# A new model of durations, with a lock for the port pair of VectorE and GpSimd, in the scheduler of an encoder block, and stage priorities chosen with it

## The chip, the cores and the metric

The kernel runs on one core of one Trainium2 chip. The metric is the device time of one launch in microseconds (us). Shorter is better. The engines are TensorE (PE in the rows; its weight loads are PEld), VectorE (DVE), ScalarE (ACT), GpSimd (POOL) and SyncE (SP), whose queue issues all the transfers of this kernel.

## The reference

One layer of a bidirectional encoder on 512 tokens of width 1024, in float32:

```python
x = layer_norm(x, ln_in_g, ln_in_b)
kern = hyena_kernels(feat, t, ...)                 # long-convolution filters from a small network
mixed = parallel_mixer(x, w_in, ...)               # branch A: GLU, depthwise conv 31, LayerNorm, silu, projection
                                                   # branch B: short conv 3, two FFT convolutions with gates, projection
                                                   # y = (g_a * y_a + g_b * y_b) @ w_mix_out
x = layer_norm(DN_ALPHA * x + mixed, ...)
xa = memory_cross_attention(x, mem, wq, wk, wv, wo)   # 4 heads, 256 memory tokens
x = layer_norm(DN_ALPHA * x + xa, ...)
moe = expert_choice_moe(x, w_router, w_gate, w_up, w_down)  # 16 experts, 64 tokens each, width 2048
x = layer_norm(DN_ALPHA * x + moe, ...)
```

The experts' weights are 16 x 3 matrices of 1024 x 2048, 403 MB in all.

## The kernel before

The program is not emitted in the order in which it is written. `body` records every operation (class `Recorder`) with a tag that names its stage; `prepare` gives each an estimated duration (`_cost`) and a critical-path length `bl`; `simulate` is a list scheduler that walks through modelled time and gives each free engine the ready operation of the highest key; `replay` then emits the instructions in that order, each engine in its own queue. As `replay` emits everything from one line, all rows of the profile carry that line (L518 before, L558 after). The names in the rows are buffers: `v` a virtual tile, `h` a piece of a host unit, `ident`, `ones`, `iota` constants.

The key of an operation is

```python
o.key = -o.i if o.late else 1e6 + o.bl - 1e-4 * o.i + prio.get(o.tag, 0)
```

so the table `PRIO` shifts whole stages, and the late part, the experts, runs in the order of the code. Some operations have alternatives (`alts`). `vg` lets an elementwise operation on two SBUF tiles go to VectorE or GpSimd, and `cp` lets a copy go to ScalarE or VectorE; `elsewhere` decides whether the engine at hand should leave the operation to the other. `split` makes the two halves of a number for three-product matmuls: a copy (`cp`) into the high half, then a subtraction (on VectorE if the source is PSUM, else by `vg`).

The stages that matter here, by their tags:

- memory keys `mt`, `mk0` to `mk7`; input LayerNorm `l0` to `l3`; filter network `fn`; filters `k00` to `k11`; DFT matrices `kd`, `df`.
- hyena inputs `c8.*`, `c0.*`; forward transforms and products in the frequency domain `f00` to `f11`, inverses `i00` to `i11`; the short convolution of the second gate `x0` to `x3`.
- GLU `g0` to `g3`; depthwise convolution `d0` to `d3`: per channel tile 24 SCALAR_TENSOR_TENSOR of about 500 columns on VectorE (`SIDE` = 3 taps on either side go to ScalarE, whose results GpSimd adds, five additions per tile); its LayerNorm `cl`.
- sixteen sigmoid gates `t0` to `t15`, each a product with a 1024 x 128 piece of `w_in`, whose weights are split first and whose result is stored to DRAM.
- projections of the two branches `b8` to `b15` (hyena) and `b0` to `b7` (conformer), eight products of 12 matmuls each; mixing `mx0`, `mx1`; LayerNorm `lm*`; values `mu`, `mv0`, `mv1`; attention `q*`, `s*`, `p*`, `o*`; output projection `wo0`, `wo1`; router `r00` to `r31`; top-k and what follows `tk`.

Every piece of weights that goes through `weight` is loaded by SP, split into a ring of four units, and used by TensorE. The expert stage streams 384 loads of 1 MB through the units of SBUF that are free; an expert needs 24. The first of these loads are issued before the front part is over, as units come free, and the rest as TensorE gives units back.

Of the kernel before, what the change touches and what calls it, by code (L numbers as in the profile page):

```python
# [31 lines left out]
PRIO = {"": 32, "b0": -50, "b1": -429, "b10": 94, "b11": -35, "b12": 27, "b13": -31, "b14": 62, "b2": -500, "b3":  # L32
# [60 lines left out]
class Op:  # L93
    __slots__ = ("i", "alts", "rd", "wr", "preds", "succ", "bl", "key", "tiles", "late", "tag", "claims")
# [78 lines left out]
def _free(ap):  # L173
    n = 1
    for st, c in list(ap.ap)[1:]:
        n *= c
    return n


def _cost(alt, psum):  # L180
    eng, meth, args, kw = alt
# [3 lines left out]
    if eng == "SP":  # L185
        b = 4 * int(np.prod([c for _, c in o.ap]))
        return b / 360e3
    if meth == "matmul":
        n = _free(o)
        r32 = x.dtype == F32R  # L190
        c = n / 2400 if r32 else max(4 * n, 512) / 2400
        k, m = x.shape[0], _free(x)
        return c / 2 if not r32 and (k == 64 or m == 64) else c
# [12 lines left out]
    return 0.068 + n * 1.0417e-3 + 0.06 * ptr  # L206

# [53 lines left out]
def prepare(rec):  # L261
# [32 lines left out]
    for op in ops:  # L294
        psum = any(v.cls in "BP" for v, _ in op.rd + op.wr)
        op.alts = [(a[0], _cost(a, psum), a) for a in op.alts]
    for op in reversed(ops):
        e = op.alts[0][0]
        tail = max([s.bl + min(_lat(e, f[0]) for f in s.alts) for s in op.succ.values()] or [0.0])
        op.bl = min(c for _, c, _ in op.alts) + tail + (2.0 if e == "SP" else 0.0)  # L300
# [4 lines left out]
def simulate(rec, prio, n=None):  # L305
# [32 lines left out]
    table, dma = [0], [0.0]  # L338
# [30 lines left out]
    def elsewhere(o, a, t):  # L369
        mine = t + o.alts[a][1]  # L370
        for b, (f, c, _) in enumerate(o.alts):
            if b != a:
                w = max(free[f], t, rtime[o.i][b]) + c
# [9 lines left out]
    def start(o, a, t):  # L383
# [11 lines left out]
        else:  # L395
# [5 lines left out]
            if e == "PE":  # L401
# [4 lines left out]
                c = c + 0.003 if clock[1] else 2 * c  # L406
                w, x = clock[0], t
                while x < t + c:
                    y = min(t + c, (w + 1) * WINDOW)
                    busy[w] = busy.get(w, 0.0) + y - x  # L410
                    w, x = w + 1, y
            fin = t + c
# [1195 lines left out]
```

## Time and profile before

| what | value |
| --- | --- |
| time before, median of 3 runs | 1681.75 us (1680.91 to 1682.41) |
| time of the profiled execution | 1678.9 us |
| its span, first to last instruction | 1677.1 us |
| busy TensorE / VectorE / ScalarE / GpSimd | 1481.5 / 739.6 / 278.0 / 273.7 us |
| granted TensorE clock, mean | 0.953 |
| bytes moved by transfers | 474.41 MB |

A row of the profile gives the busy time of a group of instructions, the mean of one, and the idle time of its engine just before them with what ended it. Outside the span lie 1.8 us of the profiled execution.

### The profile page before, as it was taken

What the parts mean: (1) busy time and instruction counts of PE and PEld (TensorE: products, weight loads), DVE (VectorE), ACT (ScalarE), POOL (GpSimd) and SP (SyncE); (2) the same over time, 40 slices, a digit from 0 to 9 for tenths busy, and PEclk for the clock granted to TensorE, in tenths of its full rate; (3) what the DMA queues carried; (4) which work ended last, traced back from release to release, by engine and by line L of the source; (5) the groups of instructions that cost most, each with busy time, mean ns of one, the idle gap of its engine ahead of it and who ended that gap; (6) DMA issues with size and microseconds to landing.
All of it is one profiled execution on the core that took longest, in us unless ns stands there. A gap on an engine that the chain in (4) does not pass through costs nothing.

```text
span 1677.1 us, 17272 instructions
## 1 busy us (share of the span) xinstructions
PE 1481.5 (88%) x6998; PEld 806.1 (48%) x6998; DVE 739.6 (44%) x1018; ACT 278.0 (17%) x465; POOL 273.7 (16%) x161
## 2 busy tenths in 40 slices
PE   7789886687899998699999999999989989988885
PEld 5678674466777887543443434324224224222222
DVE  7998999879767654603111111101101111110115
ACT  3323252123113232111100100001001001000001
POOL 3662467745101000002000000000000000000002
PEclk9889998788999998899999999999999999999997
DMA  8312221223623335579999999999999999999993
GB/s 293 130 50 90 99 64 53 67 76 107 200 89 125 114 134 209 222 301 421 415 415 419 417 415 417 418 415 416 419 415 415 420 416 414 419 417 415 418 409 149
DMA packets 99319, 474.41 MB, mean 283 GB/s; under 512 B 8449, under 2 KB 8961, under 8 KB 66344
## 3 DMA queue, kind: packets, MB, share of 16 engines
q1 hardware_dynamic: 99240, 473.31, 71.6%
q8 instruction: 55, 0.90, 0.2%
q14 instruction: 24, 0.20, 0.0%
HBM read 463.84 MB, written 9.44 MB: 282 GB/s over the span
## 4 chain that ended last, share of the span: by engine, by line
PE 52%; DMA 23%; DVE 18%; issue 3%; POOL 2%; ACT 1%; SPq 0%; DVEq 0%; ACTq 0%; POOLq 0%
PE v L518 52%; DVE v L518 14%; DMA v<-in_moe_w_down_dram 10%; DMA v<-in_moe_w_gate_dram 6%; DMA v<-in_moe_w_up_dram 6%; DVE h L518 4%; POOL v L518 2%; ACT v L518 1%; ACT h L518 0%; POOL h L518 0%; DMA h<-in_mem_dram 0%; DMA h<-in_conf_out_dram 0%; DMA h<-in_w_in_dram 0%; SPq L518 0%; DVEq L1604 0%
## 5 line engine op out<-in xcount | busy, mean ns | idle before, releaser
L518 PE MATMUL v<-v,v 128*64 128x512 f32 (+5 forms) x6370 | 1395.7, 487 | 117.5 <-DMA v<-in_moe_w_down_dram 30.4
L518 PEld LDWEIGHTS v<-v,v 128*128 128x128 f32 (+2 forms) x6370 | 729.7, 168 | 750.6 <-issue 440.2
L518 DVE TENSOR_TENSOR v<-v,v 128x512 f32<-128x512 f32 (+3 forms) x263 | 213.4, 841 | 695.0 <-PE v L518 629.3
L518 ACT ACTIVATE v<-v 128x512 fp32r<-128x512 f32 (+6 forms) x168 | 99.8, 598 | 925.3 <-PE v L518 889.0
L518 POOL TENSOR_TENSOR v<-v,mhalf 128x1 f32<-128x1 f32 (+2 forms) x21 | 15.6, 771 | 1101.3 <-DVE v L518 1101.3
L518 POOL TENSOR_TENSOR v<-h,v 128x1024 fp32r<-128x1024 f32 (+1 forms) x35 | 104.7, 2997 | 43.4 <-ACT v L518 39.3
L518 DVE SCALAR_TENSOR_TENSOR v<-v,v,v 128x499 f32<-128x499 f32 (+14 forms) x116 | 109.2, 1003 | 1.9 <-ACT v L518 1.8
L518 DVE TENSOR_TENSOR v<-h,v 128x1024 fp32r<-128x1024 f32 (+2 forms) x81 | 94.0, 1172 | 23.5 <-ACT v L518 20.9
L518 ACT ACTIVATE v<-h 128x1024 fp32r<-128x1024 f32 (+2 forms) x78 | 73.9, 961 | 131.9 <-PE v L518 89.9
L518 POOL TENSOR_TENSOR v<-v,v 128x512 f32<-128x512 f32 (+3 forms) x19 | 44.8, 2365 | 144.7 <-ACT v L518 89.9
L518 ACT ACTIVATE v<-v,v 128x128 f32<-128x128 f32 (+1 forms) x72 | 30.5, 494 | 149.2 <-PE v L518 125.8
L518 ACT ACTIVATE h<-v,v 128x512 f32<-128x512 f32 (+4 forms) x68 | 42.5, 660 | 68.7 <-PE v L518 61.3
L518 PE MATMUL v<-ident,v 128*128 128x128 f32 (+1 forms) x292 | 44.4, 287 | 9.7 <-DVE v L518 9.5
L518 DVE TENSOR_TENSOR v<-v 128x512 f32<-128x512 f32 (+4 forms) x50 | 50.6, 1056 | 1.2 <-POOL v L518 1.1
L518 PEld LDWEIGHTS v<-ident,v 128*128 128x128 f32 (+1 forms) x292 | 33.2, 145 | 36.5 <-issue 27.2
L518 PE MATMUL v<-ident,h 128*128 128x128 f32 (+1 forms) x116 | 19.4, 320 | 32.6 <-DVE h L518 20.2
L518 POOL TENSOR_TENSOR h<-h 128x256 f32<-128x256 f32 (+4 forms) x29 | 43.5, 1507 | 25.3 <-ACT h L518 17.2
L518 DVE TENSOR_SCALAR v<-iota,v,v 128x128 f32<-128x128 f32 x64 | 18.4, 343 | 63.9 <-PE v L518 63.9
L518 DVE CAST v<-h 128x1024 fp32r<-128x1024 f32 (+1 forms) x36 | 25.9, 725 | 25.1 <-PE v L518 14.9
L518 DVE COPY v<-v 128x256 f32<-128x256 f32 (+1 forms) x33 | 14.3, 433 | 47.2 <-ACT v L518 43.8
L518 PEld LDWEIGHTS v<-ident,h 128*128 128x128 f32 (+1 forms) x116 | 17.0, 184 | 35.2 <-issue 18.7
L518 DVE SCALAR_TENSOR_TENSOR v<-v,v 128x512 f32<-128x512 f32 (+1 forms) x28 | 16.9, 620 | 34.9 <-PE v L518 34.8
(67 smaller groups left out, 403.3 us busy)
## 6 DMA issues: line engine op xcount, KB each, us to landing
v<-in_moe_w_gate_dram SPq DMA_DIRECT2D x128, 1024.0 KB, 19.9
v<-in_moe_w_up_dram SPq DMA_DIRECT2D x128, 1024.0 KB, 20.0
v<-in_moe_w_down_dram SPq DMA_DIRECT2D x128, 1024.0 KB, 20.2
h<-in_w_in_dram SPq DMA_DIRECT2D x36, 512.0 KB, 3.6
v<-h SPq DMA_DIRECT2D x20, 256.0 KB, 2.1
h<-in_wk_dram SPq DMA_DIRECT2D x8, 512.0 KB
v<-v SPq DMA_DIRECT2D x8, 512.0 KB
v<-v SPq DMA_DIRECT2D x4, 1024.0 KB, 6.6
```

The source lines that it names most:

```text
L518: getattr(engs[e], meth)(*[fix(x) for x in args], **{k: fix(x) for k, x in kw.items()})
```

## The change

Four things change in the planner; `body`, `replay` and the work itself stay.

1. `_cost`: a transfer is priced at 418 instead of 360 bytes per ns, a float32r matmul 13 ns longer, a float32 one 6 ns longer (and 3 ns less in `simulate`).
2. A lock. `_shares` tells which alternatives use the port pair that VectorE and GpSimd have in common: on GpSimd every operation with two wide operands or more, on VectorE those with two inputs outside PSUM and copies and TENSOR_SCALARs between SBUF tiles. `simulate` keeps the time at which the lock is free, and an operation that shares it starts its work then.
3. `elsewhere` adds the wait for the lock to the cost of the engine at hand, and a penalty `GPEN` per tag to the GpSimd alternative; 1000 keeps a stage off GpSimd.
4. `PRIO` has new values (two lines of some thirty are shown).

```diff
-PRIO = {"": 32, "b0": -50, "b1": -429, "b10": 94, "b11": -35, "b12": 27, "b13": -31, "b14": 62, "b2": -500, "b3":
+PRIO = {"": 5334.6553, "b0": -4277.89, "b1": -5870.442, "b10": 1996.3081, "b11": 2057.3843, "b12": -8116.7025,
...
+GPEN = {"b0": 1000, "b10": -1.2595, "b13": 2.5939, "b14": 1000, "b2": 1000, "b4": 1000, "b5": 1000, "b6": 2.4193,
...
-        return b / 360e3
+        return b / 418e3
...
-        c = n / 2400 if r32 else max(4 * n, 512) / 2400
+        c = n / 2400 + 0.013 if r32 else max(4 * n, 512) / 2400 + 0.006
...
+def _shares(alt):
+
+    eng, meth, args, kw = alt
+    wide = [y for y in args if isinstance(y, bass.AP) and _free(y) > 2]
+    if eng == "G":
+        return len(wide) > 1
+    if eng != "V" or len(wide) < 2:
+        return False
+    src = [y for y in wide[1:] if y.tensor.name not in _BANKS]
+    if meth in ("tensor_tensor", "scalar_tensor_tensor", "match_replace"):
+        return len(src) > 1
+    return meth.startswith(("tensor_scalar", "tensor_copy")) and len(src) == 1 and wide[0].tensor.name not in _BANKS
...
     def elsewhere(o, a, t):
-        mine = t + o.alts[a][1]
+        pen = GPEN.get(o.tag, 0.0)
+        mine = t + o.alts[a][1] + (max(0.0, port[0] - t) if o.port[a] else 0.0)
+        mine += pen if o.alts[a][0] == "G" else 0.0
         for b, (f, c, _) in enumerate(o.alts):
             if b != a:
-                w = max(free[f], t, rtime[o.i][b]) + c
+                w = max(free[f], t, rtime[o.i][b]) + c + (pen if f == "G" else 0.0)
...
-                c = c + 0.003 if clock[1] else 2 * c
+                c = c if clock[1] else 2 * c
...
+            if o.port[a]:
+                c += max(0.0, port[0] - t)
+                port[0] = t + c
```

What this does to the program, counted over its operations. Call first part all stages up to the end of `cl` and `i11` (everything that precedes the projections of the branches). In it 76 elementwise operations move from GpSimd to VectorE (28 of 1024 columns into float32r, 28 of 512 float32, 12 of 256, 4 of 512 into float32r, 4 of 1024 float32), and 14 move from VectorE to GpSimd (3 of 1024, 5 of 512 float32, 2 of 512 into float32r, 4 of 256). Copies: 19 move from VectorE to ScalarE (8 of 1024, 10 of 512, 1 of 256), 9 the other way (6 of 1024, 3 of 512). GpSimd's tile operations there go from 113 to 51: 7 of 1024, 20 of the depthwise convolution, 12 of 512, 12 of 256. In the part from the projections to the router GpSimd has 4 before and 4 after. In the late part 9 operations of 512 go from GpSimd to VectorE, four of them in the last LayerNorm.

GpSimd's queue in the depthwise convolution, before. The 128x511 to 128x509 rows are its additions; the 128x1024 rows are the subtractions of `split` for weights of `t` and `x` stages, in the ring buffers `v401`, `v321`, `v409`, `v324`, `v373`:

```order
L518 TENSOR_TENSOR h20_80<-h20_80,h21_85 128x510
L518 TENSOR_TENSOR v401_1767<-h24_82,v401_1767 128x1024
L518 TENSOR_TENSOR h20_80<-h20_80 128x509
L518 TENSOR_TENSOR v321_1795<-h23_78,v321_1795 128x1024
L518 TENSOR_TENSOR h20_80<-h20_80 128x509
L518 MEMSET h22_87 128x1
L518 TENSOR_TENSOR h22_87<-h22_87,h21_85 128x511
L518 TENSOR_TENSOR v409_1843<-h24_82,v409_1843 128x1024
L518 TENSOR_TENSOR h22_87<-h22_87,h21_85 128x510
L518 TENSOR_TENSOR h22_87<-h22_87,h20_80 128x510
L518 TENSOR_TENSOR v324_1883<-h23_78,v324_1883 128x1024
```

The same queue after, at the end of that stage:

```order
L558 TENSOR_TENSOR h21_122<-h21_122,h22_132 128x509 x2
L558 MEMSET h21_122 128x1
L558 TENSOR_TENSOR h21_122<-h21_122,h20_80 128x511
L558 TENSOR_TENSOR h21_122<-h21_122 128x510
L558 TENSOR_TENSOR h21_122<-h21_122,h22_132 128x510
L558 TENSOR_TENSOR v330_2048<-h23_78,v330_2048 128x1024
L558 TENSOR_TENSOR h21_122<-h21_122,h22_132 128x509
L558 TENSOR_TENSOR h21_122<-h21_122,h20_80 128x509
L558 TENSOR_TENSOR v397_2140<-h23_78,v397_2140 128x1024
```

Of the weight splits in this stage two are left on GpSimd, `v330` (stage `x3`) and `v397` (stage `t1`). The others stand on VectorE, between the SCALAR_TENSOR_TENSORs of the convolution (`v266` is its result; `v413`, `v417` are ring buffers of `t` stages):

```order
L558 SCALAR_TENSOR_TENSOR v266_1858<-v265_1651,v0_111,v266_1858 128x503
L558 TENSOR_TENSOR v413_2231<-h23_78,v413_2231 128x1024
L558 SCALAR_TENSOR_TENSOR v266_1858<-v265_1651,v0_111,v266_1858 128x503
L558 SCALAR_TENSOR_TENSOR v266_1858<-v265_1651,v0_111,v266_1858 128x506
L558 SCALAR_TENSOR_TENSOR v266_1858<-v265_1651,v0_111,v266_1858 128x502
L558 SCALAR_TENSOR_TENSOR v266_1858<-v265_1651,v0_111,v266_1858 128x505
L558 SCALAR_TENSOR_TENSOR v266_1858<-v265_1651,v0_111,v266_1858 128x502
L558 SCALAR_TENSOR_TENSOR v266_1858<-v265_1651,v0_111,v266_1858 128x505
L558 SCALAR_TENSOR_TENSOR v266_1858<-v265_1651,v0_111,v266_1858 128x501
L558 TENSOR_TENSOR v417_2270<-h23_78,v417_2270 128x1024
```

TensorE's queue at the projections, before. Products with `v348` and `v355` are the hyena branch's (`b8` to `b15`), those with `v444` and `v445` the conformer's (`b0` to `b7`):

```order
L518 MATMUL v429_2772<-v355_2722,v428_2764 128x512
L518 MATMUL v486_2811<-v444_2683,v483_2782 128x512
L518 MATMUL v486_2811<-v445_2693,v483_2782 128x512
L518 MATMUL v486_2811<-v444_2683,v483_2782 128x512 x2
L518 MATMUL v486_2811<-v445_2693,v483_2782 128x512
L518 MATMUL v486_2811<-v444_2683,v483_2782 128x512 x2
L518 MATMUL v486_2811<-v445_2693,v483_2782 128x512
L518 MATMUL v486_2811<-v444_2683,v483_2782 128x512 x2
L518 MATMUL v433_2827<-v348_2567,v432_2820 128x512 x2
```

After, all hyena products stand ahead of the conformer's, and the matmuls of `cl` (with `ones`) among them:

```order
L558 MATMUL v433_2750<-v355_2703,v432_2724 128x512
L558 MATMUL v455_2777<-ones_70,h20_80 128x1 x4
L558 MATMUL v433_2750<-v355_2703,v432_2724 128x512 x5
L558 MATMUL v430_2726<-v355_2703,v428_2719 128x512 x2
L558 MATMUL v459_2796<-h20_80,ones_70 128x128 x4
L558 MATMUL v430_2726<-v355_2703,v428_2719 128x512 x2
L558 MATMUL v429_2806<-v348_2643,v428_2719 128x512 x6
L558 MATMUL v429_2806<-v355_2703,v428_2719 128x512 x6
L558 MATMUL v442_2826<-v348_2643,v441_2753 128x512 x6
```

In the late part SP issues its 392 transfers in the same order as before, and TensorE's products follow the order of the code more closely (gathers of later experts no longer stand inside the products of an earlier one).

## Rows read from the trace of the kernel before

**Rows 1.** The page: span, busy time of three engines with their share and count, and transfers in 40 equal slices of 41.9 us.

```profile
span 1677.1 us, 17272 instructions
...
PE 1481.5 (88%) x6998; PEld 806.1 (48%) x6998; DVE 739.6 (44%) x1018; ACT 278.0 (17%) x465; POOL 273.7 (16%) x161
...
GB/s 293 130 50 90 99 64 53 67 76 107 200 89 125 114 134 209 222 301 421 415 415 419 417 415 417 418 415 416 419 415 415 420 416 414 419 417 415 418 409 149
```

**Rows 2.** Busy time of each engine in five stretches: the first part, the projections, mixing to top-k, experts, the end. Columns: stretch, its length, busy us of PE, PEld, DVE, ACT, POOL with counts, granted TensorE clock, DMA share, GB/s.

```profile
0.00:432.00 432.00, 341.68 (x1662) 279.81 (x1662) 389.86 (x441) 136.08 (x189) 241.89 (x136) 0.89 0.32 105
432.00:484.00 52.00, 46.14 (x196) 36.41 (x197) 39.14 (x53) 7.59 (x9) 3.52 (x2) 1.00 0.45 148
484.00:715.60 231.60, 206.69 (x1013) 170.22 (x1013) 142.14 (x236) 53.16 (x110) 10.74 (x10) 0.93 0.43 155
715.60:1640.00 924.40, 870.27 (x3996) 310.13 (x3998) 145.84 (x250) 77.36 (x152) 8.42 (x5) 0.99 1.01 412
1640.00:1677.10 37.10, 16.70 (x134) 9.56 (x130) 22.57 (x40) 3.80 (x6) 9.13 (x8) 0.79 0.31 118
```

**Rows 3.** The chain that ended last, at the projections and before top-k. Columns: start us, length us, what.

```profile
432.30 3.66 DMA h<-in_conf_out_dram
...
436.82 42.52 PE v L518 x183
...
481.27 1.30 DVE v L518 x2
...
482.60 1.23 DVE v L518
...
483.88 5.29 PE v L518 x15
```

```profile
695.78 1.86 DVE v L518 x10
```

**Rows 4.** Instructions in order of time around the start of the expert stage: TensorE's first gather product, and SP's issues (start us, time until the last of the group was issued).

```profile
715.64 1.65 PE L518 MATMUL v<-v,v 128*128 128x128 f32 x6 [1.04 <-DVE v L518]
```

```profile
693.85 36.76 SPq L518 DMA_DIRECT2D v<-in_moe_w_gate_dram  x8
732.00 14.10 SPq L518 DMA_DIRECT2D v<-in_moe_w_down_dram  x8
```

**Rows 5.** VectorE's instructions by shape in 0 to 432 us. Columns: names, shapes, count, busy us, mean ns of one, idle time before them.

```profile
L518 DVE TENSOR_TENSOR v<-v 128x512 f32<-128x512 f32 x32 | 36.2, 1176 | 1.2 <-POOL v L518 1.1
...
L518 DVE TENSOR_TENSOR v<-v,v 128x1024 f32<-128x1024 f32 x12 | 27.6, 2350 | 0.1
L518 DVE SCALAR_TENSOR_TENSOR v<-v,v,v 128x507 f32<-128x507 f32 x8 | 14.9, 1865 | 0.0
...
L518 DVE TENSOR_TENSOR v<-h,v 128x512 fp32r<-128x512 f32 x15 | 14.7, 1002 | 2.4 <-PE v L518 1.5 <-ACT v L518 0.7
...
L518 DVE SCALAR_TENSOR_TENSOR v<-v,v,v 128x508 f32<-128x508 f32 x8 | 11.7, 1464 | 1.0 <-ACT v L518 1.0
...
L518 DVE SCALAR_TENSOR_TENSOR v<-v,v,v 128x504 f32<-128x504 f32 x8 | 11.1, 1398 | 0.0
L518 DVE TENSOR_TENSOR h<-v,h 128x512 f32<-128x512 f32 x16 | 10.6, 680 | 0.7 <-PE v L518 0.7
L518 DVE TENSOR_TENSOR h<-h,h 128x512 f32<-128x512 f32 x8 | 10.5, 1315 | 0.7 <-ACT h L518 0.7
...
L518 DVE TENSOR_TENSOR v<-v 128x1024 f32<-128x1024 f32 x8 | 9.7, 1213 | 0.0
...
L518 DVE SCALAR_TENSOR_TENSOR v<-v,v,v 128x500 f32<-128x500 f32 x8 | 5.8, 730 | 0.0
```

**Rows 6.** GpSimd's instructions in 0 to 432 us by operands: min/median/max ns of one, first and last start, shapes; and one group by shape (as in rows 5).

```profile
L518 POOL TENSOR_TENSOR v<-h,v x33: 1287/2700/17238, 20.9 to 423.6; 128x1024 fp32r<-128x1024 f32 x28, 128x512 fp32r<-128x512 f32 x5
...
L518 POOL TENSOR_TENSOR h<-h,h x16: 1277/1596/2142, 61.5 to 396.1; 128x510 f32<-128x510 f32 x7, 128x512 f32<-128x512 f32 x4, 128x511 f32<-128x511 f32 x3, 128x509 f32<-128x509 f32 x2
L518 POOL TENSOR_TENSOR v<-v x14: 1182/1298/1779, 162.1 to 398.5; 128x512 f32<-128x512 f32 x12, 128x256 f32<-128x256 f32 x2
```

```profile
L518 POOL TENSOR_TENSOR h<-h 128x256 f32<-128x256 f32 x18 | 18.3, 1030 | 7.9 <-DVE h L518 7.3 <-POOL h L518 0.2
```

**Rows 7.** Instructions in order of time in the depthwise convolution, and the first two waits of VectorE. Columns: start us, length us, instruction, count, in brackets the idle time before it and what ended it.

```profile
305.38 23.95 DVE L518 SCALAR_TENSOR_TENSOR v<-v,v,v 128x511 f32<-128x511 f32 x33 [0.54 <-ACT v L518]
...
314.29 19.57 POOL L518 TENSOR_TENSOR v<-h,v 128x1024 fp32r<-128x1024 f32 x2 [4.38 <-ACT v L518]
...
331.58 16.67 PE L518 MATMUL v<-v,v 128*128 128x512 f32 x60 [14.25 <-POOL v L518]
...
345.38 1.23 DVE L518 TENSOR_TENSOR v<-h,v 128x1024 fp32r<-128x1024 f32 x1 [16.05 <-ACT v L518]
```

```profile
4.48 0.69 DVE L518 CAST v<-h 128x1024 fp32r<-128x1024 f32 x1 [4.48 <-DMA h<-in_wk_dram]
...
10.02 0.69 DVE L518 TENSOR_TENSOR v<-v,v 128x512 fp32r<-128x512 f32 x1 [3.59 <-ACT v L518]
```

**Rows 8.** Instructions in order of time in the last LayerNorm.

```profile
1662.51 6.49 POOL L518 TENSOR_TENSOR v<-v,v 128x512 f32<-128x512 f32 x4
...
1662.96 1.58 DVE L518 TENSOR_TENSOR v<-v,v 128x512 f32<-128x512 f32 x1
...
1666.13 3.41 DVE L518 TENSOR_TENSOR v<-v,v 128x512 f32<-128x512 f32 x2
```

More of the change, by code (lines that the diff above doesn't have):

```diff
@@ L93 @@
 class Op:
-    __slots__ = ("i", "alts", "rd", "wr", "preds", "succ", "bl", "key", "tiles", "late", "tag", "claims")
+    __slots__ = ("i", "alts", "rd", "wr", "preds", "succ", "bl", "key", "tiles", "late", "tag", "claims", "port")
 class Engine:
@@ L206, in _cost @@
     return 0.068 + n * 1.0417e-3 + 0.06 * ptr
+def _shares(alt):
[9 more added lines that the diff above has]
+    return meth.startswith(("tensor_scalar", "tensor_copy")) and len(src) == 1 and wide[0].tensor.name not in _BANKS
+_BANKS = set()
 def _lat(a, b):
@@ L295, in prepare @@
         psum = any(v.cls in "BP" for v, _ in op.rd + op.wr)
+        _BANKS.update(v.name for v, _ in op.rd + op.wr if v.cls in "BP")
         op.alts = [(a[0], _cost(a, psum), a) for a in op.alts]
+        op.port = [_shares(a) for _, _, a in op.alts]
     for op in reversed(ops):
@@ L337, in simulate @@
     clock, busy = [0, False], {}
-    table, dma = [0], [0.0]
+    table, dma, port = [0], [0.0], [0.0]
     order, ev, rel = [], [0.0], []
```

39 rows, old and new, of tables (GPEN, PRIO) are left out of this document.

## The prediction

> **What bounds the kernel now.** Read the transfers in slices first [rows 1]: from slice 18 to the end they move 409 to 421 GB/s, a flat line, and before it half of that at most but for the first slice and the last two. The table of stretches [rows 2] says the same: 1.01 of the transfer engines in 715.6 to 1640 us, 0.32 to 0.45 before. So the kernel has a part bound by the experts' weights (924 us, 412 GB/s) and a front part of 716 us that isn't bound by transfers. Is the front hidden behind the stream? No: SP spends 36.76 us on the eight gate loads of the second expert, and the next load goes out at 732.0 [rows 4], since those units come free only when TensorE works on the first expert, after its first gather product at 715.64 [rows 4]. Whatever the front part loses or gains before 715.64 moves the end by as much.
>
> The front part has two halves. To 432 us VectorE is busy 389.9 us of 432 and TensorE 341.7 at a granted clock of 0.89 [rows 2]. From 484 to 715.6 TensorE is busy 206.7 of 231.6 [rows 2] and the last 16 us of it are top-k on VectorE. Between them stand the projections: the chain runs on TensorE from 436.82 for 42.5 us and, after a short turn over VectorE, reaches the first mixing product at 483.88 [rows 3]. So the change can act in one place above all, VectorE's first 432 us.
>
> **What VectorE's 389.9 us consist of.** Shapes whose operands leave GpSimd little to collide with have steady prices: 0.68 us for 512 columns, 1.21 for 1024, 0.73 for a step of the depthwise convolution [rows 5]. The same shapes cost more elsewhere: 32 of 512 columns 1.18, 12 of 1024 columns 2.35, convolution steps 1.87, 1.46, 1.40 [rows 5]. What exceeds the steady price is 16 us in the 32, 13.7 in the 12, 9.1, 5.9 and 5.3 in those three groups of convolution steps, 5.1 and 4.9 in two groups of TENSOR_TENSORs [rows 5]; the same subtraction over all groups of that view gives 106 us. VectorE's own work is then 390 - 106 = 284 us. GpSimd was busy 242 us meanwhile [rows 2], 232 of them in 113 tile operations, so a microsecond of GpSimd costs VectorE 106/232 = 0.46. GpSimd pays too: its 1024-column subtraction takes 17.2 us at worst against a median of 2.7 [rows 6]. That one did harm: while VectorE ran 33 convolution steps in a row, GpSimd's split waited, TensorE stood 14.25 us for it, and VectorE then 16.05 us for a copy of weights behind that [rows 7].
>
> **The change, part by part.**
>
> *Work moved onto VectorE.* 32 operations of 1024 columns at 1.21, 32 of 512 at 0.68 and 12 of 256 at 0.4 (estimate: just over half of the 512 price) come, 65 us; 3, 7 and 4 of them go, 10 us; the copies exchanged with ScalarE take off about 6 (19 go, 9 come, 0.4 to 1.2 each). That is +49 us; 52 more instructions in the queue, and neighbours overlap by some 0.06 us (32 x 1.176 is 37.6, busy 36.2 [rows 5]), so +46. Nine operations of later stages stand ahead of the last of `cl`: +7. Own work 284 + 46 + 7 = 337 us. All of this is on the path, as VectorE is what bounds this half.
>
> *Collisions, taken away and left.* GpSimd keeps 51 tile operations there: 7 of 1024 at 2.70, 20 additions at 1.60, 12 of 512 at 1.30, 12 of 256 at 1.03 [rows 6], 81 us. At 0.46 that costs VectorE 37 us; by the count, 106 x 51/113, it is 48. I take 40, near the first, as the price per microsecond is the better measure. The bounds are 0 (all of it where VectorE works from PSUM or waits) and 81 (each microsecond costs one). The Trainium skill, SBUF — State Buffer, Who interferes with whom, calls the shared port pair an exclusive lock for the whole instruction, where the second to issue waits until the first is done; by that alone each side waits for one instruction of the other at most. The 17.2 us under 33 steps [rows 6, 7] say that here GpSimd lost the pair many times in a row. By the page's rule the term has the upper bound of 81, and the sum below would come out at 487 instead of 446.
>
> *Idle time of VectorE.* It was 432 - 389.9 = 42.1 us: 8.1 at the start, for the first weights and the first copy [rows 7], 16.05 behind the starved split [rows 7], 18 in small waits. After: 8 and 18 stay, the 16 go, as the splits of that stage stand on VectorE but for two. New is about 16: the gates `t` now come before the second transforms, so TensorE has nothing to fill in during `f10` to `cl`, and its granted clock, 0.89 on average in this half [rows 2], can fall to its lower level of 1.2 GHz. I put 7 us on that (some 14 us of products of `f1*` and `i1*` that VectorE waits for, half as long again), and 9 us on the turns of `cl` over TensorE and ScalarE (two reductions, one broadcast, one sigmoid, some 2 us each), which other work covered before; both are estimates. 34 us in all beside the start; bounds 18 and 45.
>
> *The projections.* They took 484 - 432 = 52 us after VectorE had finished the first half, as all 192 products came behind it. After, the hyena branch's 96 stand ahead, among the matmuls of `cl`, and 96 remain: 96 x 42.5/183 = 22 us, with 2.6 of VectorE behind them [rows 3] and 2 for the clock, 27. Their weights' splits and products on VectorE are about as long (25 us) and lie beside.
>
> Sum for the first mixing product: before 8 + 34 + 390 + 52 = 484; after 8 + 337 + 40 + 34 + 27 = 446. **38 us earlier.**
>
> *Mixing to top-k*: the same 1,000 matmuls, four GpSimd operations before and after. At the end two more router chains stand behind the last output projection, 1.9 us each on VectorE [rows 3], but TensorE gets there earlier by the products that it leaves for later: 0, within 3 either way.
>
> *Expert stage*: SP's order is unchanged and the stream ran at its flat rate with both kinds of order on TensorE, for the first two experts stood in the new kind already: 0. In the last LayerNorm four operations on GpSimd, 6.49 us, go to VectorE at 0.68 and no longer stretch its own of 1.58 and 3.41 [rows 8]: 0. The prices of transfers and matmuls act through the order alone.
>
> So the span goes from 1677.1 to 1639, the profiled execution from 1678.9 to 1641. The median of the runs shown stands 2.85 us above that execution; 1681.75 - 38 = 1644.
>
> **Rivals.**
>
> *The split starves again.* Two splits are left on GpSimd in the convolution, `x3` and `t1`, under the same steps on VectorE. For it: the planner's lock hands over after each operation, the trace shows 33 in a row [rows 7]. Against it: VectorE's queue there is now mixed with subtractions that wait for ScalarE's copies and let GpSimd in. Price: about 15 us each (17.2 less the undisturbed 2.4, TensorE's wait of 14.25 [rows 7]): 1659 with one, 1674 with both.
>
> *Collisions nearly vanish.* The early GpSimd work falls where VectorE reads PSUM, at 10 to 15 us for the term instead of 40, and the new idle time stays away: some 40 us more, 1604 to 1612.
>
> *VectorE is only loaded more (slower).* GpSimd's work left lies in the convolution and the filters, where VectorE's steps read SBUF twice, and each microsecond costs more than one, as a VectorE instruction that loses also delays what ScalarE and TensorE wait for. The sum turns at a term of 78 us; at the 106 of before it gives 512 for the first mixing product, 28 late: 1710, and at 95, 1699. A page speaks for it in part: the Trainium skill, Perfetto Trace Analysis, Optimizing Scalar/DVE Operations, says that where VectorE is saturated offloading to other engines may make sense, and adds that between these two it may not help. VectorE at 390 of 432 us is that case, and the change goes the other way; the 106 us say that offloading didn't pay here.
>
> *No change.* The front is shorter, but the expert stream starts no earlier, because units come free late. [Rows 4] speak against it: the loads wait for the first products alone.
>
> **Chances.** The forecast, 25 to 55 us faster: 0.47. Starvation again, 4 to 25 faster: 0.21. More than 55: 0.14. No change: 0.06. Slower: 0.12. A measurement tells 0.2% (3.4 us) from no change: faster 0.82, same 0.06, slower 0.12. The range of 1612 to 1680 leaves out about 0.19: the slower case and half of the upper one. The likeliest one's own range is 1627 to 1657.
>
> **What would show it.** VectorE's busy time to the end of `cl` near 370 us; its 512- and 1024-column groups near 0.68 and 1.21; GpSimd near 80 us there, no weight split of 10 us or more; the first mixing product at 446, the first gather near 678; the stream flat from there on, 961 us to the end. Wrong would be: convolution steps above 1.2 us on average, VectorE idle over 60 us before the projections, or a dip below 409 GB/s in the expert stage.

## The result, and the profile after

The changed kernel takes 1621.88 us (median; 1619.88 to 1624.72) against 1681.33 (1680.32 to 1682.41) for the kernel before on the same chip: a ratio of 0.9648, 95% interval 0.9631 to 0.9664. That is 59.5 us less where 38 were forecast: the sign and the range held, the size didn't. Ratios in this text are against executions of the kernel before in the same session, whose medians lie between 1679.1 and 1681.3 us; in two sessions 5 of 24 of these executions took only 1669 to 1674 us, as 3 of 10 of "old, `mv0` late" below took 1668 to 1669, and since none of them was profiled the reason is open. The page of the kernel after:

```profile
span 1620.4 us, 17237 instructions
...
PE 1459.3 (90%) x6998; PEld 792.9 (49%) x6998; DVE 699.4 (43%) x1076; ACT 288.2 (18%) x478; POOL 112.7 (7%) x90
...
GB/s 306 120 64 93 103 104 136 104 69 158 78 91 169 26 337 207 229 418 414 418 418 415 418 418 415 418 418 416 417 418 415 417 419 415 418 419 415 417 408 153
```

GpSimd's 273.7 us have become 112.7, and VectorE's busy time fell by 40 us although it has 58 instructions more [rows 1]. The flat part of the transfers is as before, 414 to 419 GB/s but for the last two slices (408 in the last but one, 409 before). Next the kernel after in the five stretches of [rows 2], with the same columns (stretch, length, busy us of PE, PEld, DVE, ACT, POOL with counts, clock, DMA share, GB/s); the borders are now the end of `cl`, the first mixing product, the first gather, and 37 us from the end:

```profile
0.00:407.80 407.80, 345.44 (x1741) 288.10 (x1742) 367.15 (x502) 149.45 (x204) 96.72 (x75) 0.90 0.38 125
407.80:437.46 29.66, 26.36 (x114) 21.02 (x113) 27.30 (x43) 4.45 (x5) 0.00 (x0) 0.99 0.21 71
437.46:659.70 222.24, 204.39 (x1016) 169.49 (x1017) 141.32 (x235) 53.24 (x111) 13.33 (x11) 0.95 0.45 161
659.70:1583.40 923.70, 864.33 (x3978) 303.37 (x3980) 142.77 (x255) 77.24 (x152) 0.00 (x0) 0.99 1.01 412
1583.40:1620.40 37.00, 18.82 (x154) 10.95 (x150) 20.85 (x44) 3.81 (x6) 2.67 (x4) 0.82 0.34 131
```

Against [rows 2, 3]: the first mixing product comes at 437.46 instead of 483.88 (46.4 us earlier), the stretch from there to the first gather takes 222.2 instead of 231.8 (9.5 less), and from the first gather to the end it is 960.7 against 961.5. Together 56.7 us of span (the profiled execution of before is 2.4 us under its median, hence less than 59.5). The first two terms are nearly the whole effect, 55.9 us.

The chain that ended last around the projections (start, length, what), to be held against [rows 3]:

```profile
396.41 37.77 PE v L558 x166
...
434.20 0.70 DVE h L558
...
436.11 1.31 DVE v L558 x2
...
437.46 12.77 PE v L558 x41
```

TensorE is now on the chain from before the end of `cl`: its 166 products to 434.2 hold the last projections of both branches, in place of 183 products that began some 5 us after VectorE was through.

VectorE's instructions by shape up to 407.8 us (columns as in [rows 5]):

```profile
L558 DVE TENSOR_TENSOR v<-h,v 128x1024 fp32r<-128x1024 f32 x48 | 63.1, 1314 | 3.5 <-PE v L558 2.7 <-ACT v L558 0.5
L558 DVE TENSOR_TENSOR v<-v 128x512 f32<-128x512 f32 x44 | 33.5, 814 | 0.0
L558 DVE TENSOR_TENSOR v<-v,v 128x1024 f32<-128x1024 f32 x16 | 18.7, 1219 | 0.0
...
L558 DVE SCALAR_TENSOR_TENSOR v<-v,v,v 128x501 f32<-128x501 f32 x8 | 8.0, 999 | 0.0
...
L558 DVE SCALAR_TENSOR_TENSOR v<-v,v,v 128x508 f32<-128x508 f32 x8 | 7.3, 914 | 0.0
...
L558 DVE SCALAR_TENSOR_TENSOR v<-v,v,v 128x502 f32<-128x502 f32 x8 | 6.7, 835 | 0.0
...
L558 DVE SCALAR_TENSOR_TENSOR v<-v,v,v 128x507 f32<-128x507 f32 x8 | 5.9, 735 | 0.0
```

In [rows 5] the 512-column group cost 1176 ns each, the 1024-column one 2350, the 507-column step 1865. Now 44 of the first take less than 32 did, the second is at its steady 1.2 us, and only three groups of convolution steps are still well above 0.73 us (999, 914 and 835 ns). The splits of weights that came over (`v<-h,v`, 48 in all) cost 1.31 each.

GpSimd's splits over the same time (count, min/median/max ns, first and last start, shapes), against the 33 with a worst case of 17238 in [rows 6]:

```profile
L558 POOL TENSOR_TENSOR v<-h,v x12: 1286/2398/4935, 28.8 to 386.5; 128x1024 fp32r<-128x1024 f32 x8, 128x512 fp32r<-128x512 f32 x4
```

### The profile page after: what moved, and what is told of

It is laid out like the page before. It is cut to its first block, busy times and chain, and to the rows that moved or that the text cites. A ratio compares the mean times of both kernels' runs of the same rounds, so it can differ in the third digit from the quotient of the medians.

```text
span 1620.4 us, 17237 instructions
## 1 busy us (share of the span) xinstructions
PE 1459.3 (90%) x6998; PEld 792.9 (49%) x6998; DVE 699.4 (43%) x1076; ACT 288.2 (18%) x478; POOL 112.7 (7%) x90
## 4 chain that ended last, share of the span: by engine, by line
PE 61%; DMA 26%; DVE 7%; ACT 1%; POOL 1%; issue 0%; DVEq 0%; SPq 0%; ACTq 0%
PE v L558 61%; DMA v<-in_moe_w_up_dram 10%; DMA v<-in_moe_w_down_dram 8%; DMA v<-in_moe_w_gate_dram 6%; DVE v L558 6%; DVE h L558 1%; POOL v L558 1%; ACT v L558 1%; DMA h<-in_w_mix_dram 0%; DMA h<-in_w_in_dram 0%; ACT h L558 0%; POOL h L558 0%; DVEq L1644 0%; SPq L558 0%; ACTq L558 0%
## 5 line engine op out<-in xcount | busy, mean ns | idle before, releaser
L558 PE MATMUL v<-v,v 128*64 128x512 f32 (+5 forms) x6370 | 1376.9, 486 | 103.8 <-DMA v<-in_moe_w_down_dram 33.3
L558 PEld LDWEIGHTS v<-v,v 128*64 128x64 f32 (+2 forms) x6370 | 719.2, 167 | 728.5 <-issue 416.3
L558 ACT ACTIVATE v<-v 128x512 fp32r<-128x512 f32 (+5 forms) x175 | 104.5, 606 | 882.1 <-PE v L558 846.6
L558 DVE TENSOR_TENSOR v<-h,v 128x1024 fp32r<-128x1024 f32 (+1 forms) x101 | 119.6, 1190 | 10.4 <-PE v L558 5.0
L558 DVE SCALAR_TENSOR_TENSOR v<-v,v,v 128x498 f32<-128x498 f32 (+14 forms) x116 | 82.5, 758 | 5.4 <-ACT v L558 5.2
L558 POOL TENSOR_TENSOR v<-h,v 128x1024 fp32r<-128x1024 f32 (+1 forms) x15 | 38.8, 2586 | 146.4 <-ACT v L558 146.3
L558 PEld LDWEIGHTS v<-ident,v 128*128 128x128 f32 x292 | 32.8, 143 | 31.1 <-issue 17.8
L558 PE MATMUL v<-ident,v 128*128 128x128 f32 x292 | 43.7, 285 | 2.9 <-DVE v L558 2.9
L558 ACT ACTIVATE h<-v 128x512 f32<-128x512 f32 (+3 forms) x35 | 17.8, 514 | 102.9 <-PE v L558 102.6
L558 POOL TENSOR_TENSOR h<-h,h 128x509 f32<-128x509 f32 (+3 forms) x18 | 27.6, 1535 | 79.0 <-ACT h L558 77.5
```

Of the source, the lines that this page charges most:

```text
L558: getattr(engs[e], meth)(*[fix(x) for x in args], **{k: fix(x) for k, x in kw.items()})
```

## Experiments

Four terms recur. T is the end of `cl` or `i11`, whichever is later. VectorE's *excess* up to T is what its instructions took over their steady price (0.68 us for 512 columns, 1.21 for 1024, 0.73 for a convolution step, and so on), summed over the instructions matched one by one with the plan; that gives 110 us before, where the prediction's sum over groups gave 106. *Own* is busy time less excess, *idle* is T less busy. The last projection ends with its last operation outside TensorE, and the last column goes to the first step of top-k on VectorE. The table has all the runs; the sections after it say what each was for.

| kernel | time, us | T | own | excess | idle | GpSimd busy to T | T to last projection | from there to top-k |
| --- | --- | --- | --- | --- | --- | --- | --- | --- |
| before | 1681.3 | 431 | 279 | 110 | 42 | 242 | 51 | 218 |
| after | 1621.9 | 408 | 333 | 34 | 41 | 97 | 29 | 207 |
| old order, new engines | 1646.8 | 396 | 329 | 38 | 30 | 89 | 53 | 220 |
| new order, old engines | 1658.9 | 443 | 286 | 95 | 62 | 218 | 30 | 208 |
| 16 splits to VectorE | 1655.5 | 406 | 297 | 85 | 25 | 179 | 52 | 218 |
| 2 splits to VectorE | 1682.3 | 433 | 282 | 107 | 45 | 236 | 51 | 218 |
| GpSimd least | 1652.2 | 433 | 360 | 19 | 54 | 43 | 33 | 210 |
| no lock in the plan | 1666.8 | 426 | 337 | 47 | 42 | 99 | 53 | 210 |
| no penalties | 1695.2 | 485 | 294 | 97 | 94 | 218 | 28 | 208 |
| old priorities | 1691.8 | 444 | 311 | 59 | 74 | 160 | 54 | 218 |
| old, `mv0` late | 1676.7 | 430 | 280 | 108 | 42 | 242 | 52 | 215 |
| new, `mv0` early | 1632.2 | 407 | 334 | 34 | 40 | 96 | 29 | 219 |

### Engines alone, order alone

The kernel before with its order, but each of the 107 operations that stand on another of VectorE and GpSimd in the kernel after put there (`SWAP` maps an operation's number to its alternative); and the reverse, the kernel after with these operations put back. The copies that the change exchanges between VectorE and ScalarE (19 and 9 in the first part) are not among the 107: they go with the order in both runs.

```diff
+SWAP = {43: 0, 71: 0, 100: 1, 128: 0, 157: 0, 242: 0, 369: 0, 372: 0, 382: 1, 385: 1, 388: 0, 390: 1, 399: 1,
...
-    return sorted(order)
+    return [(t, i, SWAP.get(i, a)) for t, i, a in sorted(order)]
```

> The order of the kernel before, unchanged on every queue, with each of the 107 operations that the change moves between VectorE and GpSimd on the engine that it has after. Theory A (fewer collisions between VectorE and GpSimd are the gain): VectorE's own work rises by some 46 us to 333, collisions fall from 106 to 35, the 16 us behind the starved split go, so the first part ends 30 to 40 us earlier than 432, the projections (52 us) and the mixing part stay: 1642 to 1652 us. Theory B (the new order is the gain): no gain, 1677 to 1727, as VectorE has more of its own work.

Measured: 1646.79 us, ratio 0.9809 [0.9794, 0.9824], 32 us less. The row to the end of `i11` (columns as in [rows 2]):

```profile
0.00:395.80 395.80, 332.43 (x1646) 271.42 (x1647) 366.33 (x503) 136.55 (x188) 88.92 (x74) 0.92 0.34 113
```

The engines alone bring VectorE to the same 366 us of busy time as after (367), and it is through at 396, 12 us before the kernel after. What this kernel lacks comes later: 53 us of projections instead of 29, and 220 us to top-k instead of 207.

> The order of the kernel after with the 107 operations on the engines that they had before. Theory A: collisions return to about 106 us and own work falls by 46, so the first part ends 25 to 40 us later than 408: 1647 to 1662 us. Theory B: 1617 to 1627, as after.

Measured: 1658.93 us, 0.9886 [0.9871, 0.9901], 19 us less by the ratio (20 by the medians). VectorE is later (443 against 431) with 62 us idle, but the projections and the part behind them are as short as after. So the two halves of the change act in two places: the engines on VectorE up to T, the order (with the copies) on what lies behind T, and the order costs 12 us at T with either assignment (396 to 408, 431 to 443).

### Which work to take off GpSimd

The kernel before with only the 16 splits of 1024 columns of the `t` and `x` stages moved to VectorE, by the same code; and with only two of them, one in `x3` and one in `t6`, which I took for the pair behind which TensorE had stood 14.25 us [rows 7]. They are not that pair, as the time lines below show.

```diff
+SWAP = {1616: 0, 1646: 0, 1676: 0, 1706: 0, 1920: 0, 1949: 0, 1978: 0, 2007: 0, 2065: 0, 2094: 0, 2123: 0,
+        2181: 0, 2210: 0, 2268: 0, 2326: 0, 2355: 0}
```

> The kernel before, with only the 16 subtractions of 1024 columns in the weight splits of the t and x stages moved from GpSimd to VectorE. Theory A: 16 x 1.15 = 18 us more of own work, about 59 us of GpSimd less at 0.46 = 27 us fewer collisions, no stall of 16 us behind a starved split: 25 us faster, 1656. Theory B: 1681 to 1699. If the starved split alone matters: near 1680, since 16 won and 18 spent.

Measured: 1655.53 us, 0.986 [0.9845, 0.9874], 24 us less: these 16 operations give three quarters of what the engines alone give (14 of them are among the 76 that the change moves; the other two, in `x3` and `t1`, it leaves on GpSimd). Excess falls by 25, own work grows by 18, and idle time falls by 17: the 16 us behind the starved pair are gone.

```diff
+SWAP = {1706: 0, 2326: 0}
```

> The kernel before, its order kept; of the whole change only two subtractions of 1024 columns (one each in x3 and t6, the pair behind which TensorE stood 14.25 us and VectorE then 16.05 us) move from GpSimd to VectorE. Theory (the starved pair costs that idle time by itself): VectorE's idle time before the projections falls from 42 to 26 to 30 us, its own work grows by 2.4, and the time falls by 11 to 16 us, to 1665 to 1670. Rival (the next split left on GpSimd starves in its place, so only the move of all sixteen helps): idle time stays at 38 to 44 us and the time at 1678 to 1684.

Measured: 1682.3 us, 1.0019 [1.0002, 1.0037], within 0.2% of the kernel before. The kernel before has four weight splits in a row on GpSimd at this place. By the plan the first two are those of `t6` and `x3`, which took 5.74 us together (start, length, instruction, count, idle time before it):

```profile
304.18 5.74 POOL L518 TENSOR_TENSOR v<-h,v 128x1024 fp32r<-128x1024 f32 x2 [1.85 <-ACT v L518]
```

The starved pair behind them, at 314.29 [rows 7], is that of `t14` and `t13`. In this run `t6` and `x3` stand on VectorE and the starved pair is still on GpSimd. The time line of VectorE, then of GpSimd:

```profile
305.81 1.22 DVE L520 TENSOR_TENSOR v<-h,v 128x1024 fp32r<-128x1024 f32 x1 [0.88 <-ACT v L520]
...
308.92 1.21 DVE L520 TENSOR_TENSOR v<-h,v 128x1024 fp32r<-128x1024 f32 x1
310.06 20.91 DVE L520 SCALAR_TENSOR_TENSOR v<-v,v,v 128x504 f32<-128x504 f32 x32
347.35 1.23 DVE L520 TENSOR_TENSOR v<-h,v 128x1024 fp32r<-128x1024 f32 x1 [16.38 <-ACT v L520]
```

```profile
315.67 19.84 POOL L520 TENSOR_TENSOR v<-h,v 128x1024 fp32r<-128x1024 f32 x2 [11.93 <-ACT v L520]
```

So the time came out as the rival said, but the run tests neither the theory nor the rival. It is the same pair as before that starves: 17.50 us for its first split, 19.84 for both, and VectorE idles 16.38 us. Whether moving this pair alone would have saved the 11 to 16 us stays open. The nearest to a test is the run with 16 splits, which moves it along with 14 others: idle time fell by 17 us. What the two splits do show is that splits that don't starve are worth nothing on either engine (3 us more of own work, 3 us less excess). The first split of the pair ends 2.2 us after the last of the 32 steps: it is done when the run is over.

### As little as possible on GpSimd

The kernel after, where the plan pays 1000 us for any alternative on GpSimd.

```diff
-        pen = GPEN.get(o.tag, 0.0)
+        pen = 1000.0
```

> The kernel after with the penalty of 1000 for every stage: GpSimd keeps only the 20 additions of the depthwise convolution. 31 operations more on VectorE are 21 us of its own work; some 65 us of GpSimd less at 0.35 to 0.45 are 23 to 29 us fewer collisions: 1612 to 1625, near after. If GpSimd's remaining work was hidden (its collisions where VectorE waits anyway): 1635 to 1645.

Measured: 1652.21 us, 0.9846 [0.9813, 0.988], 30 us slower than after. Excess falls to 19 us, but own work grows to 360 and idle time to 54. Own work and excess together are 379 against 367: the last 54 us of GpSimd cost 15 us of excess and save 27 us of work. The plan also has another order here, with 13 us more of idle time and 7 us more behind T; what in it costs them was not taken apart.

### The plan's rules, one at a time

The kernel after without the lock in the plan; without the penalties; and with the old table of priorities. Each lets the planner make a new order and a new assignment.

```diff
-        op.port = [_shares(a) for _, _, a in op.alts]
+        op.port = [False for _ in op.alts]
```

> The kernel after with the lock taken out of the planner (no operation shares the pair) and the penalties and priorities kept; GpSimd gets 57 tile operations in the front instead of 55. If the price per microsecond of GpSimd (0.35 to 0.47) is what counts: 1620 to 1630, as the engines are nearly those of after. If the lock's place in the plan counts for itself, as it tells the planner when a slot is free: 1635 to 1650.

Measured: 1666.84 us, 0.9927 [0.9902, 0.9952]. GpSimd has hardly more to do than after (99 us), since the penalties keep work off it; excess is 47, idle time 42. Of the 45 us lost against after, 24 are in the projections: `i11` ends after `cl` in this order, and 53 us follow T. Another 19 are lost up to T.

```diff
-GPEN = {"b0": 1000, "b10": -1.2595, "b13": 2.5939, "b14": 1000, "b2": 1000, "b4": 1000, "b5": 1000, "b6": 2.4193,
...
+GPEN = {}
```

> The kernel after with the penalties on GpSimd taken out and the lock and priorities kept; GpSimd gets 117 tile operations again. If its amount of work is what counts: 62 operations more, some 120 us, cost 50 us of collisions and spare VectorE 46 us, and the starved or late splits come on top: 1640 to 1660. If the lock in the plan is enough: 1620 to 1630.

Measured: 1695.17 us, 1.0097 [1.0059, 1.0135]: slower than the kernel before. With the lock in the plan, but no penalty, GpSimd gets 218 us of work again. In order of time:

```profile
327.14 21.81 DVE L551 SCALAR_TENSOR_TENSOR v<-v,v,v 128x511 f32<-128x511 f32 x30 [5.10 <-ACT v L551]
...
329.81 2.94 POOL L551 TENSOR_TENSOR v<-h,v 128x1024 fp32r<-128x1024 f32 x1 [4.59 <-ACT v L551]
...
338.56 14.91 POOL L551 TENSOR_TENSOR v<-h,v 128x1024 fp32r<-128x1024 f32 x2 [5.81 <-ACT v L551]
...
351.20 13.65 PE L551 MATMUL v<-v,v 128*128 128x512 f32 x46 [11.93 <-POOL v L551]
...
371.55 2.99 DVE L551 TENSOR_TENSOR v<-v 128x512 f32<-128x512 f32 x3 [22.60 <-PE v L551]
```

Thirty steps in a row, a starved pair of splits, TensorE 11.93 us late, VectorE 22.60. A split that came early in the same run got in at once, for 2.94 us, and cost VectorE one step of 2.86 instead of 0.73; the next one lost until the run was over. What decides between the two, these records don't show. The plan's lock has each side wait for one operation of the other, as in the first case. So it doesn't see what starvation costs. That the penalties are what keeps the splits away from it in the kernel after is likely by this run, though the order differs too.

```diff
-PRIO = {"": 5334.6553, "b0": -4277.89, "b1": -5870.442, "b10": 1996.3081, "b11": 2057.3843, "b12": -8116.7025,
...
+PRIO = {"": 32, "b0": -50, "b1": -429, "b10": 94, "b11": -35, "b12": 27, "b13": -31, "b14": 62, "b2": -500, "b3":
...
```

> The kernel after with the table of priorities of before; lock, penalties and prices new. GpSimd gets 73 tile operations. From the run with old order and new engines (32 us faster) and 22 operations more on GpSimd: 1640 to 1655, with the wait of TensorE for the last head's softmax still there. If lock and prices find as good an order by themselves: 1620 to 1635.

Measured: 1691.75 us, 1.0083 [1.0051, 1.0116], slower than before too: idle time 74. GpSimd's longest splits (time line):

```profile
332.51 18.20 POOL L550 TENSOR_TENSOR v<-h,v 128x1024 fp32r<-128x1024 f32 x2 [11.48 <-ACT v L550]
...
368.27 12.23 POOL L550 TENSOR_TENSOR v<-h,v 128x1024 fp32r<-128x1024 f32 x1 [16.32 <-ACT v L550]
```

### The 9.5 us between mixing and top-k

TensorE's time line in the kernel before, at the softmax of the last head:

```profile
632.60 2.02 PE L518 MATMUL v<-ident,h 128*128 128x128 f32 x8 [4.24 <-DVE h L518]
635.31 0.79 PE L518 MATMUL v<-v,v 128*128 128x512 f32 x1 [0.69 <-ACT v L518]
636.64 8.71 PE L518 MATMUL v<-v,v 128*128 128x512 f32 x28 [0.53 <-DVE v L518]
```

It waits 5.5 us in three places, and 28 matmuls then take 8.71 us. The 20 us around it (columns as in [rows 2]), and behind it the 20 us at the same stage after:

```profile
623.88:643.88 20.00, 13.99 (x59) 10.78 (x58) 8.58 (x15) 5.27 (x13) 0.00 (x0) 0.74 0.73 288
```

```profile
577.46:597.46 20.00, 20.00 (x93) 16.34 (x92) 11.66 (x21) 4.77 (x10) 0.00 (x0) 1.00 1.02 408
```

A granted clock of 0.74 over 20 us is half clock, 1.2 GHz, for 10.2 of them (the records have it from 630.9 to 641.1). After, TensorE has products of `o0` and `o1` left, since the value product `mv0` on which they wait has a very low priority; it doesn't stand, and the clock stays at 2.4 GHz. Of the 10.2 us, 2.9 lie in the waits themselves, and in the other 7.3 TensorE does half as much, which loses 3.7 by this estimate. Waits of 5.5 and 3.7 make 9.1 us; 9.5 was measured. That the two are so close is in part chance. From the first mixing product to the first step of top-k TensorE's idle time falls from 9.5 to 2.3 us, more than the softmax's waits, and its busy time from 206.2 to 203.8, less than 3.7, as the clock is lower than before in the first 20 us of mixing (0.85 on average, 0.91 before). Two runs try this: the kernel before with `mv0` late, and the kernel after with `mv0` early.

```diff
-"mv0": -43
+"mv0": -8469.8488
```

> The kernel before with one priority changed, that of mv0 (second-half values), to its value of after. TensorE's order is the same up to the attention; then products of heads 0 and 1 come after the scores of head 3 instead of before and fill the wait for its softmax. Theory A (the 9.5 us between mixing and top-k are that wait, 4.2 us, and 10 us at the lower clock behind it): 1671 to 1674. Rival (they lie elsewhere): 1680 to 1683.

Measured: 1676.71 us, 0.997 [0.9952, 0.9988], 2.4 us less, between the two forecasts. The profile is of an execution of 1676.99:

```profile
539.50 0.66 PE L518 MATMUL v<-ident,v 128*128 128x128 f32 x4 [2.83 <-DVE v L518]
```

```profile
536.00:556.00 20.00, 17.17 (x72) 13.91 (x71) 17.55 (x21) 6.67 (x10) 4.67 (x3) 0.83 0.50 168
624.00:644.00 20.00, 17.93 (x85) 13.88 (x84) 13.74 (x24) 5.41 (x14) 0.00 (x0) 1.00 1.01 412
```

The half clock at the softmax is gone (624 to 644 at 1.00), but `mv0` is now missing where it had covered the LayerNorm after mixing: TensorE waits 2.83 us there, and 6.8 us at half clock follow. The hole has moved.

```diff
-        "mv0": -8469.8488, "mv1": 2491.1271, "mx0": 9122.1904, "mx1": -1530.2513, "o0": 3427.2784, "o1": 2009.193,
+        "mv0": 2491.1271, "mv1": 2491.1271, "mx0": 9122.1904, "mx1": -1530.2513, "o0": 3427.2784, "o1": 2009.193,
```

> The kernel after with one value of PRIO: mv0 gets the priority of mv1, as it has in effect in the kernel before. Up to the attention TensorE's order is that of after; then the value product is no longer late, and while the last head's softmax runs only four matmuls of o2 are left to TensorE. Theory (the 9.5 us between the first mixing product and top-k come from TensorE having work during the last softmax): a wait of some 4 us on VectorE's softmax comes back, with a stretch at half clock of some 10 us behind it; mixing to top-k 229 to 232 us instead of 222, and the time 1628 to 1632 instead of 1622. Rival (they come from another place of the order, the LayerNorm after mixing or the router): 220 to 224 us, and the time 1620 to 1624.

Measured: 1632.18 us, 0.9716 [0.97, 0.9732]: 10.3 us slower than after (11 by the ratios) by one number in the table, for which the planner also puts 14 operations, most of them copies, on other engines. TensorE's time line and the 20 us around it:

```profile
587.46 2.07 PE L558 MATMUL v<-ident,h 128*128 128x128 f32 x8 [3.30 <-issue]
590.32 0.80 PE L558 MATMUL v<-v,v 128*128 128x512 f32 x1 [0.78 <-DVE v L558]
592.27 21.77 PE L558 MATMUL v<-v,v 128*128 128x512 f32 x84 [1.16 <-DVE v L558]
```

```profile
577.00:597.00 20.00, 14.76 (x63) 11.57 (x62) 10.72 (x19) 5.87 (x14) 0.00 (x0) 0.74 0.74 293
```

The wait is back (5.2 us in three places), and with it the same 0.74, 10.2 us at half clock. From the first mixing product to the first gather it is now 234.8 us (436.80 to 671.63), 12.6 more than after, of which the expert stage gives 2.5 back. By the same sum waits of 5.2 and a loss of 3.7 make 9.0. The 3.6 beyond that lie in other places of the stretch: up to the first step of top-k TensorE is idle 10.3 us instead of 2.3 (new beside the softmax's are above all waits of 1.4 us at 443.5 and of 0.7 at 508.2) and busy 208.5 instead of 203.8. Why the expert stage returns 2.5 isn't explained. So by these two runs `mv0` late is needed for the gain in the new order, and is not enough in the old one.

## Why the prediction was right, and where its size was off

**What bounds the kernel: right.** What the front part gained moved the end by as much: 55.9 us until the first gather, 56.7 at the end. The expert stage is flat, 960.7 us with 961 predicted. The rival "no change" is out.

**The sum for the first mixing product: right in its terms, 8 us too cautious.** Predicted 446, measured 437.5:

| term | predicted | measured |
| --- | --- | --- |
| VectorE's own work to T | 337 | 333 |
| collisions | 40 | 34 |
| idle time with the start | 42 | 41 |
| projections | 27 | 30 |

The price of 0.46 us of VectorE for each microsecond of GpSimd carried: 34 for 97 us of GpSimd is 0.35. In the other plans of the table it is 0.37 to 0.47 (38/89 with the engines alone, 95/218, 85/179, 19/43, 47/99, 97/218, 59/160, 107/236), over a range of GpSimd's time from 43 to 236 us. GpSimd was busy 97 us to T, not the forecast 80; at the lower price the term is still smaller. VectorE was busy 367 us to T, near the 370 named as the sign. The term lies well inside its bounds of 0 and 81. Two slips in the working weigh less than 1 us each: the four groups of GpSimd's work add up to 79 us, not 81, and the overlap of neighbours is 0.04 us by its row, not 0.06.

**The idle time: right in sum, wrong in one part.** What VectorE waited for, after to 407.8 us and before to 432 (total, times, longest):

```profile
DVE v L558 <- ACT v L558: 13.3, 9, 3.8
DVE v L558 <- PE v L558: 9.4, 8, 2.7
DVE h L558 <- PE v L558: 5.1, 5, 2.1
```

```profile
DVE v L518 <- ACT v L518: 24.4, 10, 16.1
DVE v L518 <- PE v L518: 5.1, 4, 1.7
...
DVE h L518 <- PE v L518: 0.7, 1, 0.7
```

The 16.1 are gone, as forecast. Waits for TensorE grew from 5.8 to 14.5, 8.7 more where 7 were put down. The turns of `cl`, put at 9, hardly show; other small waits on ScalarE grew by 5 instead (24.4 less 16.1 is 8.3, now 13.3). The clock did fall, much further than I allowed for, but mostly where VectorE had work of its own:

```profile
340.00:360.00 20.00, 8.19 (x32) 6.91 (x32) 20.00 (x27) 3.97 (x4) 0.00 (x0) 0.50 0.19 62
360.00:380.00 20.00, 7.18 (x32) 6.15 (x32) 19.79 (x30) 5.82 (x8) 0.00 (x0) 0.59 0.69 253
380.00:396.00 16.00, 12.20 (x44) 8.86 (x44) 13.29 (x18) 5.42 (x7) 3.38 (x2) 0.72 0.45 133
```

From 340 to 380 us TensorE is at half clock for the most part and works less than half of the time, and VectorE is busy 39.8 of these 40 us. So it costs next to nothing there. Of the 2.7 us that VectorE stands idle to 396, the turns of `cl` are a part.

**"Mixing to top-k: 0, within 3 either way": the step that failed.** It is -9.5 us. A term was put at nothing, and with the 8 us above it makes up what was missing. I compared counts, the same 1,000 matmuls and as many operations on GpSimd, and looked at what stands on the end of that part (the router). The 4.24 us hole at the softmax, with the half clock behind it, stood in the trace of before and would have been found by going through TensorE's waits from 484 us on; the order of after shows that `mv0` and with it `o0` and `o1` move. The run with `mv0` early shows it the other way round: one priority put back, 10.3 us lost. Without this term the sum gives 47 us of span instead of 38, inside the likeliest case; with it 57, beyond its edge of 55.

**The rivals.** "More than 55" came true by its bound, but not by its own times (1604 to 1612) or its mechanism: collisions were to fall to 10 to 15 us and the new idle time to stay away, and they are 34, with idle time as forecast. "The split starves again" did not happen: the two splits left, in `x3` and `t1`, take 3.06 and 4.42 us. It does happen in other plans: in the one without penalties and in the one with the old priorities, pairs of splits starve for 14.9 and 18.2 us under runs of 30 and 36 convolution steps. What I said against it, that VectorE's queue there is now mixed with subtractions, fits the time line: the longest run of steps without a break is 13 in the kernel after, where it was 33.

```profile
268.94 8.56 DVE L558 SCALAR_TENSOR_TENSOR v<-v,v,v 128x500 f32<-128x500 f32 x13
```

```profile
275.34 4.42 POOL L558 TENSOR_TENSOR v<-h,v 128x1024 fp32r<-128x1024 f32 x1 [7.99 <-ACT v L558]
```

This is the split of `t1`, under that longest run. It too ended 2.3 us after the run's last step, so it lost the rest of the run like the starved ones; there was only some 2 us of it left, which is in part luck. No run changes the length of such a run by itself. "VectorE only loaded more" is out: no run has a price near 1.

**The lock.** The page cited in the prediction (the Trainium skill, SBUF — State Buffer, Who interferes with whom) gives each side a wait of one instruction of the other. The traces agree in the mean, where a microsecond of GpSimd costs VectorE less than one, and not at the extreme, where a single split on GpSimd took 17.50 us under a run of 32 steps. The other page (the Trainium skill, Perfetto Trace Analysis, Optimizing Scalar/DVE Operations) doubts that moving work between these two helps: here moving 76 operations of the first part *to* the saturated engine, and 14 away from it, gave 32 us, and moving nearly all the rest, in a new plan, lost 30.

**The plan.** Neither half of the change explains it by itself: engines 32 us, order 19, both 59.5. The remaining 8 aren't taken apart further, nor are the copies, and the new prices of transfers and matmuls were not tried by themselves; by the ratios the order gives 27 us with the new engines and 19 with the old. Why the plans without the penalties, or with the old priorities, have worse idle time (94 and 74 us) was seen only as far as the starved splits, and what the plan without the lock loses only as far as `i11` behind `cl`.

## What to carry to other kernels

Price the shared pair from the trace (here 0.35 to 0.47 us of VectorE for each microsecond of GpSimd) and look apart from that for GpSimd work which another engine waits for while VectorE runs through a long chain of steps: it may be served only when the chain is over. Before such work is moved, find out from the plan's order which operations the long ones in the time line are: here an experiment moved the pair next to the starved one. When a planner's table changes, go through TensorE's longer waits (here 2.8 to 4.2 us), in all stages, and ask whether the new order has something to fill them with, since a stretch at half clock can follow (6.8 and 10.2 us here). And the parts of a plan belong together: each of three versions with one part taken out (lock, penalties, priorities) lost 45 to 73 us against the whole.

## What the runs showed of the hardware

- A GpSimd subtraction of 1024 columns, 2.4 us undisturbed, that starts under a run of VectorE convolution steps can take until the run is over: 17.24 us (before), 17.50 (two splits moved), 12.59 (no penalties) and 15.87 (old priorities), each ending 2.2 us after the last step. One that came 9 us earlier in the same run as the 12.59 got in at once, in 2.94 us.
- In three places a short stop of TensorE came with a stretch at half clock: 10.2 us at 1.2 GHz around waits of 4.24 us (before) and 3.30 us ("`mv0` early"), and 6.8 us behind one of 2.83. By the sum above the lower clock cost 3.7 us on top of waits of 5.5.
